# Moving a recurrence's gate units from the attention phase to the scans, with one weight pool and weights laid out by group

## The chip, the cores and the metric

The kernel runs on one core of a Trainium2 chip, with its engines TensorE (PE, with its weight loads PEld), VectorE (DVE), ScalarE (ACT), GpSimd (POOL) and SyncE (SP). Each engine takes its instructions in order; SP issues every DMA of this kernel, one behind the other. The metric is the time of one execution on the device, in microseconds (us).

## The reference, cut to what matters

One layer over 2048 tokens (32 rows of 64) of width 1024, with 256 context tokens:

```python
h  = rms_norm(x, norm_g) * (1 + scale) + shift          # hc likewise for the context
q, k, v, z_a, u, z_l = split(h @ w_in, 6 parts of 512)   # w_in: 1024 x 3072
attn = neighbourhood_attention(rope(q), q, rope(k), v, k_c, v_c, rpb)   # 8 heads of 64
uc = depthwise_conv(u); ucc = depthwise_conv(u_c)        # width 4
y  = scan_forward + scan_backward of the RG-LRU          # a, b from gates of uc (64 x 64 blocks)
mix = concat([attn * silu(z_a), y * silu(z_l)]) @ w_out
out = x + gate * mix
```

The gate of the recurrence is silu(z_l), the last 512 columns of w_in; its product with y is what this change moves.

## The kernel before, in words

Float32 products are made of three float16 matmuls: the prepared tokens stand as hh (high) and hl (low), four blocks of 512 tokens each; a group of weights is loaded as float32 (raw, name wraw), its largest value found (L319, and allmax L111 to L116, which crosses the partitions by two small matmuls on PE), scaled by a power of two and split into wh (ACT, L324) and wl (DVE, L325). A projection with 128 channels on the partitions (proj_ct, L344 to L346) is 8 x 3 matmuls of 512 columns.

Phase 1 (phase1): modulation vectors, preparation of x and context (prep_in, prep), the tables of the attention's bias (tables: rp is multiplied, stored as d_r, spread to d_f, copied by ACT as te, d_t, and stored as d_e), the u projections (u_proj, with the convolution L364 to L381 on DVE), and then lru for channel groups c = 0 to 3 of 128 channels. lru makes, for two directions, the gates (L447 to L449 on PE in 5 pieces of tokens, tanh L451), exp, tanh and sqrt (L455 to L458), a product (L459) and the scan (L461 forwards, L468 backwards in three pieces); POOL adds the directions (L471) and d_y stores y (L472). Between the directions, fill runs units of the attention's gate z_a: silu_z (24 projections, tanh L479, product sz L480) and four stores d_z.

Phase 2 (phase2): heads 0 to 6, each in four quarters t (steps 4n + t), with the projections of the next head beside (proj_tc, L602 to L604). Between steps stand the units of the recurrence's gate (lru_gate): load y, silu_z, four products ry (L995, L997), store d_re. The table LU says behind which steps a unit stands; `later(LZ)` gives a unit a later priority. Head 7 and the output projection follow.

The order on each engine is settled before the run by a scheduler that goes through the program's instructions by priority and takes the earliest that its own model finds ready; pools of tiles (bufs = number of buffers of a tag) make an instruction wait for the last reader of its buffer.

In the profile PE's duration of one matmul is longer than its distance to the next one, since they overlap.

Of the kernel before, what the change touches and what calls it, by code (L numbers as in the profile page):

```python
# [17 lines left out]
D = 1024  # L18
# [13 lines left out]
CQ, CK, CV, CZA, CU, CZL = 0, 512, 1024, 1536, 2048, 2560  # L32
# [19 lines left out]
LZ = 80  # L52

LU = (0, 2, 4, 6, 8, 10, 12, 14, 16, 18, 20, 22, 24, 25, 26, 27)
# [4 lines left out]
class K:  # L59
# [93 lines left out]
    def mods(self, p):  # L153
# [20 lines left out]
        for i in range(2):  # L174
            for k in range(KC):
                w = p.tile([128, D], F32, tag="x", name="wm", bufs=12)
# [77 lines left out]
    def prep_in(self, p, src, n, tb=None):  # L254
# [37 lines left out]
    def w_tiles(self, tag, n):  # L292

        if tag == "z":
            return [self.wp["z"].tile([128, KC, 128], F16, tag=x, name=x, bufs=3) for x in ("wh", "wl")]
        if tag == "l":
            return [self.wp["l"].tile([128, KC, 128], F16, tag=x, name=x, bufs=1) for x in ("wh", "wl")]
        return [self.wp["h"].tile([128, KC, 192], F16, tag=x, name=x, bufs=2)[:, :, 0:n] for x in ("wh", "wl")]

    def wload(self, parts, tag):  # L300

        n = sum(w for _, w in parts)
        wp = self.wp["z" if tag == "z" else "h"]
        if tag == "z":
            raw = wp.tile([128, KC, n], F32, tag="raw", name="wraw", bufs=2)
        else:
            raw = wp.tile([128, KC, 192], F32, tag="raw", name="wraw", bufs=1)[:, :, 0:n]
        wv = self.a["w_in"].rearrange("(k p) n -> p k n", p=128)
        o = 0
        for c, w in parts:  # L310
            self.nc.sync.dma_start(raw[:, :, o:o + w], wv[:, :, c:c + w])
            o += w
        return raw, n, tag

    def wsplit(self, raw, n, tag, early=False):
# [7 lines left out]
        wh, wl = self.w_tiles(tag, n)  # L323
# [8 lines left out]
    def wgroup(self, parts, tag, slow=False, early=False):  # L332
        raw = self.wload(parts, tag)
# [77 lines left out]
    def lru(self, c, uc, p, fill):  # L411
# [54 lines left out]
        for o, m in ((0, CTX), (CTX + S // 2, S // 2), (CTX, S // 2)):  # L466
# [3 lines left out]
            if o:  # L470
                nc.gpsimd.tensor_tensor(F[:, o:o + m], A[:, o:o + m], F[:, o:o + m], ALU.add)  # L471
                nc.sync.dma_start(self.d_y[128 * c:128 * c + 128, o - CTX:o - CTX + m], F[:, o:o + m])  # L472
# [10 lines left out]
    def phase1(self, left, right):  # L483
# [7 lines left out]
        self.zp = self.pool(right, "z", side="right")  # L491
        self.wright = right.enter_context(ExitStack())
        self.zs = self.const.tile([128, 8], F32, name="zs")
        self.wp = {}
# [3 lines left out]
        with ExitStack() as s1:  # L498
            self.wp["z"] = self.pool(s1, "w1", bufs=2)
# [3 lines left out]
            def u_group(c, g=None):  # L503
                wh, wl, osc = g or self.wgroup([(CU + 128 * c, 128)], "z", slow=c > 1)
# [16 lines left out]
            with ExitStack() as s0:  # L521
# [3 lines left out]
                with self.tc.issue_after(self.last.ins):  # L525
                    g0 = self.wgroup([(CU, 128)], "z", early=True)
# [17 lines left out]
            za = []  # L544

            def z_group():
                c = len(za)
                g = self.wgroup([(CZA + 128 * c, 128)], "z", slow=c > 0)
                nc.vector.tensor_scalar(self.zs[:, c:c + 1], g[2], 0.5, None, ALU.mult)
                za.append(g)  # L550
            with ExitStack() as s2:
                p = self.pool(s2, "lru")
                ug[2] = u_group(2)
                z_group()

                def z_units(c, d):
                    wh, wl, _ = za[c]
                    for tb in (2 * d, 2 * d + 1):
                        z = self.silu_z(self.zp, self.bank("mm"), wh, wl, self.zs[:, c:c + 1], tb)
                        dz = self.d_z[c][tb].rearrange("p (j f x) -> p f j x", j=4, f=2)  # L560
                        for f in range(2):
                            zf = z[:, 256 * f:256 * f + 256]
                            nc.sync.dma_start(dz[:, f, 0:3], zf[:, 32:224].rearrange("p (j x) -> p j x", j=3))
                            nc.sync.dma_start(dz[:, f, 3].rearrange("p (e x) -> p e x", e=2),
                                              bass.AP(zf.tensor, zf.offset, [list(zf.ap[0]), [224, 2], [1, 32]]))
                    if d == 0 and c < 3:
                        z_group()

                for c in range(4):
                    self.lru(c, ucs[c], p, lambda d, c=c: z_units(c, d))  # L570
                    if c < 2:
                        ucs.append(u_proj(c + 2))
            self.wp["h"] = self.pool(self.wright, "w2", bufs=2, side="right")
# [156 lines left out]
    def head_w(self, n):  # L730
        return self.wload([(CQ + HD * n, HD), (CK + HD * n, HD), (CV + HD * n, HD)], "h")
# [188 lines left out]
    def phase2(self, left, right):  # L920
# [4 lines left out]
        self.wp["l"] = self.pool(self.wright, "w3", side="right")  # L925
        with ExitStack() as sg:
# [22 lines left out]
            lz = self.lru_gate()  # L949
            next(lz)  # L950
            for n in range(NH - 1):
                nxt = self.head_proj(n + 1, p, q)
                for t, _ in enumerate(self.attention(n, H, p)):
# [5 lines left out]
                    step = 4 * n + t  # L959
                    if step in LU:  # L960
                        next(lz)
                    if LU.index(step + 1) % 4 == 0 if step + 1 in LU else False:
                        next(lz)
# [5 lines left out]
            next(lz, None)  # L969
# [3 lines left out]
    def lru_gate(self):  # L973

        nc = self.nc
        for c in range(4):
            hsc = self.zs[:, 4 + c:5 + c]

            raw = self.wload([(CZL + 128 * c, 128)], "h" if c == 3 else "l")
            yield  # L980
            wh, wl, osc = self.wsplit(*raw)
            nc.vector.tensor_scalar(hsc, osc, 0.5, None, ALU.mult)
            for tb in range(4):
                with self.later(LZ):
                    y = self.wp["l"].tile([128, 512], F32, tag="y", name="y", bufs=1)
                    nc.sync.dma_start(y, self.d_y[128 * c:128 * c + 128, 512 * tb:512 * tb + 512])
                    z = self.silu_z(self.zp, self.bank("mm"), wh, wl, hsc, tb)
                    w1 = self.zp.tile([128, 512], F32, tag="z", name="ry", bufs=2)
                    for f in range(2):
                        s = slice(256 * f, 256 * f + 256)  # L990
                        yf = y[:, s].rearrange("p (r c) -> p c r", r=4)
                        zf = z[:, s].rearrange("p (c r) -> p c r", r=4)
                        wf = w1.rearrange("p (i f c r) -> p f i c r", i=4, f=2, r=4)[:, f]
                        iv = lambda x: x[:, 8:56].rearrange("p (i c) r -> p i c r", i=3)
                        nc.vector.tensor_tensor(wf[:, 0:3], iv(zf), iv(yf), ALU.mult)  # L995
                        ev = lambda x: bass.AP(x.tensor, x.offset, [list(x.ap[0]), [56 * x.ap[1][0], 2], [x.ap[1][0], 8], list(x.ap[2])])
                        nc.vector.tensor_tensor(wf[:, 3].rearrange("p (e c) r -> p e c r", e=2), ev(zf), ev(yf), ALU.mult)  # L997
                    nc.sync.dma_start(self.d_re[tb][128 * c:128 * c + 128, :], w1)
                yield


    def room(self):

        return self.wp["h"].tile([128, KC, 192], F32, tag="raw", name="wo", bufs=1).rearrange("p k n -> p (k n)")[:, 0:D]
# [135 lines left out]
```

## Time and profile before

| | |
|---|---|
| median of 3 runs | 1279.6 us (1273.95 to 1280.06) |
| profiled execution | 1277.88 us, its span 1276.1 us |
| mean granted TensorE clock | 0.936 of full speed |
| PE busy | 1122.0 us (88%) |
| DVE busy | 926.6 us (73%) |
| ACT busy | 615.2 us (48%) |
| POOL busy | 478.7 us (38%) |

Busy times are sums over the span; how far an engine limits the kernel differs by stage, so the rows below take the span apart. The 40 slices of the page (31.9 us each) show PE's busy share in tenths:

```profile
PE   7777889689981879999999999999999976999997
DVE  7798655989775677888978989798887863544432
```

The scans begin in slice 7 and end in slice 13; the attention of heads 0 to 6 fills slices 14 to 33.

### The profile page before, as it was taken

Reading aid. Unit: us, or ns where it says so; the run is one execution under the profiler, and the core shown is the slowest. Engines: PE = TensorE matmul, PEld = TensorE weight load, DVE = VectorE, ACT = ScalarE, POOL = GpSimd, SP = SyncE. Lnnn points to the kernel's source line nnn. Section 1 sums busy time; section 2 is a strip of 40 time slices with the busy share of each in tenths; the row PEclk is TensorE's granted clock in tenths of the full one; section 3 lists DMA queues with packets and bytes.
Section 4 is the critical chain, followed back from the end, with each engine's and each line's share of the span. In section 5 each row is a group of like instructions: output and inputs, shape, how many; then the busy total and the mean of one; then the engine's idle time right before and its main releaser. Section 6 shows DMA issues by size and latency. Waiting matters only on the chain. (4 is left out here: it accounts for less than half of the span.)

```text
span 1276.1 us, 26205 instructions
## 1 busy us (share of the span) xinstructions
PE 1122.0 (88%) x9964; PEld 858.8 (67%) x9964; DVE 926.6 (73%) x2546; ACT 615.2 (48%) x1189; POOL 478.7 (38%) x863
## 2 busy tenths in 40 slices
PE   7777889689981879999999999999999976999997
PEld 1434345445540767889878898788887755778786
DVE  7798655989775677888978989798887863544432
ACT  1597116876773225555655555555556452231210
POOL 0144002234122087566566556565564552000000
PEclk9788899699996889999999999999999997999999
DMA  9846980011024414344543435334354346346452
GB/s 349 284 153 237 312 250 26 4 50 54 17 67 99 93 34 85 83 97 96 118 88 83 95 86 137 82 89 76 86 129 103 89 99 177 95 134 176 122 149 83
DMA packets 196014, 149.50 MB, mean 117 GB/s; under 512 B 129453, under 2 KB 168109, under 8 KB 195887
## 3 DMA queue, kind: packets, MB, share of 16 engines
q1 hardware_dynamic: 195887, 147.82, 43.3%
q8 instruction: 78, 1.28, 0.4%
q14 instruction: 49, 0.40, 0.1%
HBM read 96.42 MB, written 47.94 MB: 113 GB/s over the span
## 5 line engine op out<-in xcount | busy, mean ns | idle before, releaser
L602 PE MATMUL mm<-wh,hh 128*128 128x192 f16 x960 | 236.9, 247 | 0.0
L603 PE MATMUL mm<-wl,hh 128*128 128x192 f16 x960 | 236.9, 247 | 0.0
L604 PE MATMUL mm<-wh,hl 128*128 128x192 f16 x960 | 236.9, 247 | 0.0
L893 DVE TENSOR_TENSOR Pl<-pt,Ph 128x384 f16<-128x384 f32 (+1 forms) x256 | 127.4, 516 | 56.2 <-ACT Ph L892 55.7
L344 PE MATMUL mm<-hh,wh 128*128 128x512 f16 x384 | 150.3, 392 | 12.9 <-DVE sz L480 7.6
L345 PE MATMUL mm<-hl,wh 128*128 128x512 f16 x384 | 149.2, 389 | 8.3 <-POOL hl L289 7.9
L885 ACT ACTIVATE SP<-SP,nb 128x640 f32<-128x640 f32 (+1 forms) x128 | 110.7, 881 | 91.9 <-DVE nb L883 87.7
L346 PE MATMUL mm<-hh,wl 128*128 128x512 f16 x384 | 149.0, 388 | 0.0
L892 ACT CAST Ph<-pt 128x384 f16<-128x384 f32 (+1 forms) x256 | 107.1, 453 | 67.5 <-PE pt L891 66.6
L891 PE MATMUL pt<-id,SP 128*128 128x128 f32 x704 | 115.6, 282 | 0.6 <-ACT SP L885 0.2
L602 PEld LDWEIGHTS <-hh 128*128 128x128 f16 x1024 | 100.6, 98 | 3.6 <-issue 2.8
L603 PEld LDWEIGHTS <-hh 128*128 128x128 f16 x1024 | 100.5, 98 | 1.8 <-issue 0.3
L604 PEld LDWEIGHTS <-hl 128*128 128x128 f16 x1024 | 100.5, 98 | 1.0
L880 DVE CUSTOM_DVE_ANT_0 SP<-sl,b,m 128x384 f32<-128x384 f32 (+1 forms) x128 | 93.2, 735 | 6.6 <-PE sl L828 4.5
L828 PE MATMUL sl<-qk,qt 128*128 128x128 f16 (+2 forms) x800 | 78.2, 230 | 16.9 <-DVE m L880 6.9
L898 PEld LDWEIGHTS <-Ph 128*128 128x128 f16 x1408 | 79.1, 97 | 9.9 <-ACT Ph L892 3.1
L891 PEld LDWEIGHTS pt<-id,SP 128*128 128x128 f32 x704 | 78.9, 143 | 5.2 <-ACT SP L885 1.2
L443 POOL TENSOR_TENSOR ul<-uc,uh 128x512 fp32r<-128x512 f32 (+1 forms) x20 | 33.0, 1679 | 123.3 <-ACT uh L442 123.3
L346 PEld LDWEIGHTS <-wl 128*128 128x128 f16 x416 | 41.6, 100 | 55.4 <-issue 16.9
L717 POOL TENSOR_TENSOR ST<-P,ST 128x256 f16<-128x256 f32 x64 | 43.4, 679 | 93.7 <-ACT ST L716 93.2
L898 PEld LDWEIGHTS <-Pl 128*128 128x128 f16 x704 | 65.8, 98 | 16.1 <-DVE Pl L893 9.8
L345 PEld LDWEIGHTS <-wh 128*128 128x128 f16 x416 | 41.9, 101 | 50.3 <-issue 14.0
(303 smaller groups left out, 3060.9 us busy)
## 6 DMA issues: line engine op xcount, KB each, us to landing
b<-d_e SPq DMA_DIRECT2D x32, 288.0 KB
wm<-w_mod SPq DMA_DIRECT2D x16, 512.0 KB
x<-x SPq DMA_DIRECT2D x16, 512.0 KB
wraw<-w_in SPq DMA_DIRECT2D x12, 512.0 KB
d_t<-te SPq DMA_DIRECT2D x12, 512.0 KB
d_e<-d_t SPq DMA_DIRECT2D x8, 768.0 KB
wraw<-w_in SPq DMA_DIRECT2D x24, 256.0 KB
b<-d_e SPq DMA_DIRECT2D x16, 384.0 KB
```

The costliest lines, as they stand in the source:

```text
L344: nc.tensor.matmul(out, wh[:, k, :], hh[:, k, :n], start=(k == 0), stop=False)
L345: nc.tensor.matmul(out, wh[:, k, :], hl[:, k, :n], start=False, stop=False)
L346: nc.tensor.matmul(out, wl[:, k, :], hh[:, k, :n], start=False, stop=(k == KC - 1))
L602: nc.tensor.matmul(out, hh[:, k, t0:t0 + 128], wh[:, k, :], start=(k == 0), stop=False)
L603: nc.tensor.matmul(out, hh[:, k, t0:t0 + 128], wl[:, k, :], start=False, stop=False)
L604: nc.tensor.matmul(out, hl[:, k, t0:t0 + 128], wh[:, k, :], start=False, stop=(k == KC - 1))
L880: nc.vector.tensor_tensor_reduce(SP[:, 0:W], sl[:, 0:W], bt[:, CT[j], 0:W], self.qs, m1, ALU.add, ALU.max, accum_out=m2)
L885: nc.scalar.activation(SP[:, :N], SP[:, :N], AF.Exp, bias=nb)
L891: nc.tensor.transpose(pt[:, i - c0, :], SP[:, 128 * i:128 * i + 128], self.id32)
L892: nc.scalar.copy(Ph[:, c0:c1], pt)
L893: nc.vector.tensor_tensor(Pl[:, c0:c1], pt, Ph[:, c0:c1], ALU.subtract)
L898: nc.tensor.matmul(pv[:, jj], P[:, i, :], v[:, w:w + 66], start=(i == j0 == 0), stop=(i == nch - 1 and j0 == 2))
```

## The change

- lru_gate(c, tb, wh, wl) is now one unit, called from fill in phase 1: fill(c, d) runs z_unit(c, tb) for two blocks and, from group 1 on, lru_gate(c − 1, tb) for the same blocks. The four units of group 3 follow behind lru(3). LU, LZ and their calls in phase 2 are gone.
- The weights of z_a, u, z_l and of the heads come from one pool, w: raw has one buffer, wh and wl three, all of 8 x 192 columns. Before, phase 1 had raw two and wh, wl three (8 x 128), phase 2 one and two, and the gate's units their own.
- The host lays w_in out as w_gr (12 groups of 128 columns: each partition has one row of 4 KB) and w_qkv (8 heads: one row of 6 KB); a head's weights are one DMA in place of three.
- d_y is one tile per group; y and ry have a pool of their own with one buffer each; x and wm have 11 buffers, not 12.
- In the code, u group 3's weights and the z groups are asked for behind lru(c), and the first z_a group without the wait of slow.

```diff
-LZ = 80
-LU = (0, 2, 4, 6, 8, 10, 12, 14, 16, 18, 20, 22, 24, 25, 26, 27)
...
-        self.d_y = d.tile([LW, S], F32, name="d_y")
+        self.d_y = [d.tile([128, S], F32, name=f"d_y{c}") for c in range(4)]
...
-            x = p.tile([128, D], F32, tag="x", name="x", bufs=12)
+            x = p.tile([128, D], F32, tag="x", name="x", bufs=11)
...
+    def wload(self, src):
+        n = src.shape[2]
+        raw = self.wp.tile([128, KC * 192], F32, tag="raw", name="wraw", bufs=1)[:, 0:KC * n].rearrange("p (k n) -> p k n", k=KC)
+        self.nc.sync.dma_start(raw, src)
+        return raw, n
...
+        wh, wl = [self.wp.tile([128, KC * 192], F16, tag=x, name=x, bufs=3)[:, 0:KC * n].rearrange("p (k n) -> p k n", k=KC)
+                  for x in ("wh", "wl")]
...
+            def z_group(gs, k0, slow=True):
+                c = len(gs)
+                g = self.wgroup((GZL if k0 else GZA) + c, slow=slow)
+                nc.vector.tensor_scalar(self.zs[:, k0 + c:k0 + c + 1], g[2], 0.5, None, ALU.mult)
+                gs.append(g)
...
+                ug[2] = u_group(2)
+                z_group(za, 0, False)
+                def fill(c, d):
                     for tb in (2 * d, 2 * d + 1):
+                        z_unit(c, tb)
+                        if c:
+                            self.lru_gate(c - 1, tb, *zl[c - 1][:2])
                 for c in range(4):
+                    self.lru(c, ucs[c], p, lambda d, c=c: fill(c, d))
                     if c < 2:
                         ucs.append(u_proj(c + 2))
+                    if c < 3:
+                        z_group(za, 0)
+                        if c == 0:
+                            ug[3] = u_group(3)
+                        z_group(zl, 4)
+            z_group(zl, 4)
+            for tb in range(4):
+                self.lru_gate(3, tb, *zl[3][:2])
+            zright.close()
...
     def head_w(self, n):
-        return self.wload([(CQ + HD * n, HD), (CK + HD * n, HD), (CV + HD * n, HD)], "h")
+        return self.wload(self.a["w_qkv"][n])
...
-                    step = 4 * n + t
-                    if step in LU:
-                        next(lz)
-                    if LU.index(step + 1) % 4 == 0 if step + 1 in LU else False:
-                        next(lz)
...
+    def lru_gate(self, c, tb, wh, wl):
+        y = self.yp.tile([128, 512], F32, tag="y", name="y", bufs=1)
+        nc.sync.dma_start(y, self.d_y[c][:, 512 * tb:512 * tb + 512])
+        z = self.silu_z(self.zp, self.bank("mm"), wh, wl, self.zs[:, 4 + c:5 + c], tb)
+        w1 = self.yp.tile([128, 512], F32, tag="ry", name="ry", bufs=1)
...
+    w = np.asarray(inputs["w_in"]).reshape(KC, 128, 3 * D).transpose(1, 0, 2)
+    arrays["w_qkv"] = np.ascontiguousarray(w[:, :, :3 * AW].reshape(128, KC, 3, NH, HD).transpose(3, 0, 1, 2, 4).reshape(NH, 128, KC, 3 * HD))
+    arrays["w_gr"] = np.ascontiguousarray(w[:, :, 3 * AW:].reshape(128, KC, 12, 128).transpose(2, 0, 1, 3))
```

In the order of instructions the change shows at two places. First, VectorE where group 2 ends and group 3 begins. Before (L452 is the first product of a group's gates, L468 the backward scan of group 2, L480 a unit's sz):

```order
L480 SCALAR_TENSOR_TENSOR sz<-sz,mm 128x512
L459 TENSOR_TENSOR X<-X,I 128x2304
L480 SCALAR_TENSOR_TENSOR sz<-sz,mm 128x512
L452 SCALAR_TENSOR_TENSOR I<-I,uc 128x256
L452 SCALAR_TENSOR_TENSOR I<-I,uc 128x512
L468 SCALAR_TENSOR_TENSOR A<-A,X 128x256
L468 SCALAR_TENSOR_TENSOR A<-A,X 128x1024 x2
L452 SCALAR_TENSOR_TENSOR I<-I,uc 128x512 x3
```

The L452 rows around the scan belong to group 3, whose first gates are already done. After, with lines 18 lower (L450 is the scan, L462 sz, L351 the convolution of a u group, L300 the largest weight):

```order
L462 SCALAR_TENSOR_TENSOR sz<-sz,mm 128x512
L450 SCALAR_TENSOR_TENSOR A<-A,X 128x256
L450 SCALAR_TENSOR_TENSOR A<-A,X 128x1024 x2
L300 TENSOR_REDUCE wm<-wraw 128x1
L462 SCALAR_TENSOR_TENSOR sz<-sz,mm 128x512
L110 TENSOR_REDUCE av<-po 1x1
L973 TENSOR_TENSOR ry<-sz,y 128x3x64
L975 TENSOR_TENSOR ry<-sz,y 128x64
L973 TENSOR_TENSOR ry<-sz,y 128x3x64
L975 TENSOR_TENSOR ry<-sz,y 128x64
L351 SCALAR_TENSOR_TENSOR uc<-mm,cw_2042,uc 128x255
L357 COPY cy_2532<-mm 128x1
```

Behind the scan of group 2 now stands the convolution of u group 3; the first L434 (the product L452 of before) of group 3 comes 70 rows further down, and on PE 288 projections of 512 columns and 24 of 256 stand between the last gate of group 2 and the first of group 3.

Second, SP behind the last stores of y. Before (y and z are loads, b the tables' loads, wraw a head's weights):

```order
L472 DMA d_y<-A 128x1024 x2
L931 DMA rope<-rope 128x768
L311 DMA wraw<-w_in 128x8x64 x3
L690 DMA b<-d_e_1025 64x1152 x2
L690 DMA b<-d_e_1026 64x1536 x2
L986 DMA y<-d_y 128x512
L843 DMA z<-d_z_68 128x512
L311 DMA wraw<-w_in 128x8x64 x3
```

After:

```order
L926 DMA rope<-rope 128x768
L686 DMA b<-d_e_1028 64x1152
L293 DMA wraw<-w_qkv 128x1536
L686 DMA b<-d_e_1028 64x1152
L686 DMA b<-d_e_1029 64x1536 x2
L839 DMA z<-d_z_68 128x512
L976 DMA d_re_91<-ry 128x512
L964 DMA y<-d_y_95 128x512
L976 DMA d_re_88<-ry 128x512
L964 DMA y<-d_y_95 128x512
```

The loads of y and the stores d_re of groups 2 and 3 now stand between the loads for head 0 and the weights of head 1.

## Rows read from the trace of the kernel before

**Rows 1.** Windows by stage: span, busy us, (instructions) of each engine, clock, DMA share.

```profile
0.00:207.50 207.50, 163.75 (x696) 77.48 (x697) 149.22 (x356) 91.57 (x150) 46.44 (x51) 0.88 0.75 247
207.50:420.10 212.60, 156.48 (x682) 89.51 (x681) 167.46 (x175) 144.90 (x180) 53.57 (x52) 0.85 0.19 50
420.10:1052.00 631.90, 598.84 (x7474) 528.22 (x7474) 519.12 (x1838) 334.05 (x778) 367.73 (x752) 0.98 0.41 91
```

**Rows 2.** Windows, channel groups 0 to 3 and the stretch to head 0.

```profile
207.50:262.10 54.60, 40.97 (x163) 26.51 (x162) 47.97 (x60) 41.78 (x56) 11.70 (x7) 0.81 0.05 15
262.10:312.90 50.80, 44.41 (x204) 25.37 (x203) 43.69 (x39) 37.76 (x47) 17.31 (x8) 0.90 0.17 45
312.90:362.70 49.80, 47.77 (x220) 25.48 (x219) 40.50 (x44) 36.44 (x48) 11.67 (x7) 1.00 0.13 32
362.70:401.70 39.00, 22.17 (x96) 11.47 (x93) 31.88 (x22) 27.35 (x28) 7.07 (x3) 0.83 0.20 54
401.70:420.10 18.40, 1.16 (x4) 0.68 (x5) 3.41 (x13) 1.57 (x1) 5.83 (x29) 0.50 0.85 209
```

**Rows 3.** Timeline of PE: start, duration, line, tiles, [idle before <-releaser].

```profile
206.96 0.47 PE L447 MATMUL sl<-uh,gh 128*128 128x256 f32 x1
...
339.76 0.40 PE L449 MATMUL sc<-uh,gl 128*128 128x512 f32 x1
...
382.14 0.39 PE L449 MATMUL sc<-uh,gl 128*128 128x512 f32 x1
382.37 0.39 PE L345 MATMUL mm<-hl,wh 128*128 128x512 f16 x1
...
387.78 0.38 PE L346 MATMUL mm<-hh,wl 128*128 128x512 f16 x1
...
420.14 0.26 PE L602 MATMUL sl<-wh,hhc 128*128 128x128 f16 x1 [2.42 <-ACT wh L324]
```

**Rows 4.** Timeline of DVE around the last scans of groups 2 and 3.

```profile
357.22 5.46 DVE L468 TENSOR_TENSOR_SCAN A<-A,X 128x256 f32<-128x256 f32 x3
...
396.24 5.46 DVE L468 TENSOR_TENSOR_SCAN A<-A,X 128x256 f32<-128x256 f32 x3
414.38 1.75 DVE L319 TENSOR_REDUCE wm<-wraw 128x1 f32<-128x1536 f32 x1 [12.68 <-DMA wraw<-w_in]
...
417.75 0.16 DVE L116 COPY am<-mm 128x1 f32<-128x1 f32 x1 [0.67 <-PE mm L114]
```

**Rows 5.** Timeline of SP behind the last scan: DMA issues.

```profile
407.05 3.29 SPq L311 DMA_DIRECT2D wraw<-w_in  x3
...
413.34 0.53 SPq L986 DMA_DIRECT2D y<-d_y  x1
```

**Rows 6.** Windows, the 12 steps of phase 2 without a unit: their sum.

```profile
sum 220.59, PE 213.60 PEld 196.07 DVE 179.63 ACT 118.91 POOL 114.15; mean PE 17.80 PEld 16.34 DVE 14.97 ACT 9.91 POOL 9.51
```

**Rows 7.** The same for the 15 steps with a unit.

```profile
sum 316.09, PE 308.90 PEld 263.33 DVE 272.03 ACT 180.51 POOL 202.53; mean PE 20.59 PEld 17.56 DVE 18.14 ACT 12.03 POOL 13.50
```

**Rows 8.** Lines of DVE, 420 to 1052 us: count | busy us, mean ns | idle before.

```profile
L995 DVE TENSOR_TENSOR ry<-sz,y 128x192 f32<-128x192 f32 x32 | 21.7, 678 | 0.0
...
L997 DVE TENSOR_TENSOR ry<-sz,y 128x64 f32<-128x64 f32 x32 | 15.4, 483 | 0.0
...
L480 DVE SCALAR_TENSOR_TENSOR sz<-sz,mm 128x512 f32<-128x512 f32 x16 | 10.8, 677 | 0.0
```

**Rows 9.** Timeline of DVE, the tables' first product and block 0.

```profile
50.82 0.62 DVE L632 TENSOR_SCALAR rp<-rp,acols 120x31 f32<-120x31 f32 x1
...
64.86 0.41 DVE L287 CAST hh<-h 128x512 f16<-128x512 f32 x1
```

**Rows 10.** Lines of DVE, 207 to 420 us: the convolution of two u groups.

```profile
L369 DVE SCALAR_TENSOR_TENSOR uc<-us,cw,uc 128x512 f32<-128x512 f32 (+2 forms) x24 | 22.9, 958 | 0.2
...
L364 DVE TENSOR_SCALAR uc<-us,cw,vec 128x512 f32<-128x512 f32 x8 | 7.5, 953 | 0.7 <-ACT us L362 0.6
```

**Rows 11.** The chain of waits: start, us, what it waited for.

```profile
1124.11 3.27 DMA m<-d_at
```

More of the change, by code (lines that the diff above doesn't have):

```diff
@@ L289, in prep, with wsplit @@
             self.hl_op = eng.tensor_tensor(hl[:, k, :], h[:, :m], hh[:, k, :], ALU.subtract)
[L292 to L315, printed above, removed]
+    def wload(self, src):
[3 more added lines that the diff above has]
+        return raw, n
+    def wsplit(self, raw, n, early=False):
         nc = self.nc
@@ L330, in wsplit, with wgroup @@
         return wh, wl, osc
-    def wgroup(self, parts, tag, slow=False, early=False):
-        raw = self.wload(parts, tag)
+    def wgroup(self, g, slow=False, early=False):
+        raw = self.wload(self.a["w_gr"][g])
         with ExitStack() as st:
@@ L471, in lru @@
                 nc.gpsimd.tensor_tensor(F[:, o:o + m], A[:, o:o + m], F[:, o:o + m], ALU.add)
-                nc.sync.dma_start(self.d_y[128 * c:128 * c + 128, o - CTX:o - CTX + m], F[:, o:o + m])
+                nc.sync.dma_start(self.d_y[c][:, o - CTX:o - CTX + m], F[:, o:o + m])
     def silu_z(self, p, pz, wh, wl, hsc, tb):
@@ new lines, in z_unit @@
+            def z_unit(c, tb):
+                z = self.silu_z(self.zp, self.bank("mm"), *za[c][:2], self.zs[:, c:c + 1], tb)
+                dz = self.d_z[c][tb].rearrange("p (j f x) -> p f j x", j=4, f=2)
+                for f in range(2):
+                    zf = z[:, 256 * f:256 * f + 256]
+                    nc.sync.dma_start(dz[:, f, 0:3], zf[:, 32:224].rearrange("p (j x) -> p j x", j=3))
+                    nc.sync.dma_start(dz[:, f, 3].rearrange("p (e x) -> p e x", e=2),
+                                      bass.AP(zf.tensor, zf.offset, [list(zf.ap[0]), [224, 2], [1, 32]]))
@@ L551, in phase1 @@
             with ExitStack() as s2:
                 p = self.pool(s2, "lru")
+                self.yp = self.pool(zright, "y", side="right")
                 ug[2] = u_group(2)
-                z_group()
-                def z_units(c, d):
-                    wh, wl, _ = za[c]
+                z_group(za, 0, False)
+                def fill(c, d):
                     for tb in (2 * d, 2 * d + 1):
[L559 to L567, printed above, removed]
+                        z_unit(c, tb)
+                        if c:
+                            self.lru_gate(c - 1, tb, *zl[c - 1][:2])
@@ L968, in phase2 @@
             self.out_weights(range(4, 8), self.room)
-            next(lz, None)
         self.wright.close()
         return self.attention(NH - 1, H, p)
-    def lru_gate(self):
+    def lru_gate(self, c, tb, wh, wl):
         nc = self.nc
[L976 to L999, printed above, removed]
@@ new lines, in lru_gate @@
+        y = self.yp.tile([128, 512], F32, tag="y", name="y", bufs=1)
+        nc.sync.dma_start(y, self.d_y[c][:, 512 * tb:512 * tb + 512])
+        z = self.silu_z(self.zp, self.bank("mm"), wh, wl, self.zs[:, 4 + c:5 + c], tb)
+        w1 = self.yp.tile([128, 512], F32, tag="ry", name="ry", bufs=1)
+        for f in range(2):
+            s = slice(256 * f, 256 * f + 256)
+            yf = y[:, s].rearrange("p (r c) -> p c r", r=4)
+            zf = z[:, s].rearrange("p (c r) -> p c r", r=4)
+            wf = w1.rearrange("p (i f c r) -> p f i c r", i=4, f=2, r=4)[:, f]
+            iv = lambda x: x[:, 8:56].rearrange("p (i c) r -> p i c r", i=3)
+            nc.vector.tensor_tensor(wf[:, 0:3], iv(zf), iv(yf), ALU.mult)
+            ev = lambda x: bass.AP(x.tensor, x.offset, [list(x.ap[0]), [56 * x.ap[1][0], 2], [x.ap[1][0], 8], list(x.ap[2])])
+            nc.vector.tensor_tensor(wf[:, 3].rearrange("p (e c) r -> p e c r", e=2), ev(zf), ev(yf), ALU.mult)
@@ L1002, in room @@
+        nc.sync.dma_start(self.d_re[tb][128 * c:128 * c + 128, :], w1)
     def room(self):
-        return self.wp["h"].tile([128, KC, 192], F32, tag="raw", name="wo", bufs=1).rearrange("p k n -> p (k n)")[:, 0:D]
+        return self.wp.tile([128, KC * 192], F32, tag="raw", name="wo", bufs=1)[:, 0:D]
     def out_weights(self, ks, room):
```

29 lines of the change are left out of this document (9 added, 20 removed).

## The prediction

> **What bounds the kernel now.** I read the busy time by stage first. From the first gate of the recurrence (about 207 us) to the first projection of head 0 (420.1 us) TensorE is busy 156.48 of 212.60 us and VectorE 167.46. In the attention of heads 0 to 6 (420 to 1052) TensorE is busy 598.84 of 631.90 [rows 1]. So the attention is bound by TensorE, and the stage of the scans is bound by neither: there the three engines wait for each other. The same view by channel group shows where TensorE idles [rows 2]: 13.6, 6.4, 2.0 and 16.8 us in groups 0 to 3, then 17.2 of the 18.4 us between the last scan and head 0. Second, the timeline of TensorE: a gate matmul of 512 columns takes 0.23 us to the next instruction (382.14 to 382.37), projections of 512 columns follow each other every 0.216 us (25 of them from 382.37 to 387.78) [rows 3]. One unit of a recurrence gate is 24 such projections, 5.2 us; the 16 units together are 384, or 82.9 us. Third, VectorE's timeline: the last scan of group 2 ends at 362.7 and of group 3 at 401.7, and after that head 0 waits for its weights to land (12.68 us) and for their split [rows 4]. SP issues those weights at 407.05, behind the last stores of y [rows 5].
>
> **What phase 2 gives back.** The table puts a unit into 15 of the 27 whole (head, quarter) steps that follow the first. Step by step from the second reciprocal of one (L901) to that of the next, the 12 steps without a unit have TensorE busy 213.60 of 220.59 us (6.99 idle) and the 15 steps with one 308.90 of 316.09 (7.19 idle) [rows 6, 7]. Idle per step is 0.58 without and 0.48 with. The units fill no idle time here, they lengthen the phase, so without them it is shorter by nearly all of 82.9 us. I take off 3 us for 15 steps that become a little worse: **−80**. The bounds are −86 (VectorE, busy 519 of 632 us there [rows 1], also loses L995, L997 and L480, 47.9 us [rows 8]) and −48, which is VectorE's share alone, if VectorE turned out to pace these steps.
>
> **What the scans' stage now carries.** Four steps.
>
> *Up to the first gate: +3 (from −5 to +16).* The x tiles have 11 buffers in place of 12, and the raw weights one in place of two. The product rp, whose store d_r opens the chain of the bias tables, ran on VectorE at 50.82 us, before block 0 of the prepared x; in the new order it stands behind the third cast of that block, which ended at 65.3 [rows 9], and d_r stands on SP behind x tiles that wait for buffers: some 14 to 18 us later, 16 by the middle. The tables are not read before head 0, but ScalarE copies them (te) between its other work. I pass on 3 of the 16 and keep 16 as the upper bound; below, 5 us, since the last loads wg and the store d_g now stand earlier on SP. Weights in rows of 4 KB in place of 512 B can only land sooner; the one wait for weights that these rows show is head 0's, so I count nothing for it here.
>
> *First gate to the last gate of group 2: 0 (from −16 to +7).* It was 206.96 to 340.15 us [rows 3], 133.2. VectorE is busy 132.2 of the 155 us of groups 0 to 2 [rows 2]. It loses the convolution of u group 3 (22.9 + 7.5 us for two groups [rows 10], so 15.2), which now stands behind the scans of group 2. It gains three ry products with their sz (2.3 + 0.7 us each, from the sums of [rows 8] over 16 units) and two splits of weights of about 3 us: 15 us. Even, therefore. The low bound has VectorE busy 95% of this stretch in place of 85 (139 us against 155), the high one 82% as in group 3.
>
> *Last gate of group 2 to the last scan of group 3: +69 (from +64 to +77).* Before, it was 340.15 to 401.7, 61.5 us. In the order after, 288 projections of 512 columns and 24 of 256 stand on TensorE between the last gate of group 2 and the first of group 3: u group 3, which used to stand in front of those gates, and eight units. 288 x 0.216 + 24 x 0.11 = 64.8 us, with no gate in them, so neither ScalarE nor VectorE can begin group 3. Between this gate and the last gate of group 3 stand 168 more: 36.3 us, and the 60 gate matmuls take 12.3. Then tanh, exp, sqrt, product and scan, which took 19.2 us from 382.5 to 401.7; I take 17, since one sz fewer stands among them. Sum 130.4, against 61.5. It is paced by TensorE, so waits can only add, up to 8 us as I take it from the 16.8 idle of group 3 before; the low end is a chain of 12 us in place of 17 behind the last gate.
>
> *Last scan to head 0: +21 (from +15 to +25).* It was 18.4 us [rows 2]. Now the split of head 0's weights stands on VectorE behind the last ry, and the units of group 3 stand behind a wait. Their largest weight is reduced (av) only after the last scan, so their first projection starts about 8 us after it; four units take 20.8, so TensorE is through at +29. The ry chain runs beside it: y has one buffer and ry one, so each round is product 2.3, issue of d_re and y 0.4 each, landing 3.3 (a quarter-megabyte load of d_at took 3.27 [rows 11]): 6.4 us. y(3,0) is issued behind d_y, rope, the tables b, the head's weights and d_re(2,3), at about +11, and lands between +14.4 and +18.4 behind the head's weights, which took 7.3 us [rows 5, 4]; I take +16. Product, three more rounds and the split (2.4 us from L116 to the first projection [rows 4, 3]): 16 + 2.3 + 19.2 + 2.4 = 39.9. Loading the head's weights by one DMA in place of three saves 2.9 of 3.29 us on SP, which is in the +11. The tiles d_y by group take no wait away that a row shows.
>
> Sum: +3 + 0 + 69 + 21 − 80 = **+13** on the profiled execution (span 1276.1 and 1.8 us around it, 1277.9), 1291. The median of the runs is 1.7 above that, so 1292. In other words: 82.9 us of units, and 69 projections of 512 and 24 of 256 columns of u groups that used to stand in front of the first gate (17.5 us), come into a stage that grows by 90 us, so only some 10 of its 56 us of idle time are filled: the units stand in one lump and at the tail, not in the gaps.
>
> **Rivals.**
>
> *Faster: the units sink into the idle time.* TensorE idles 56 us between 207.5 and 420.1, 39 of it beside the scans [rows 1, 2]. If its order lets 39 of the 82.9 us sink in, and the tail stays at 18.4, head 0 starts 44 later, and −80 makes it −36: about 1244. For it: group 0 and group 3 have 13.6 and 16.8 us of idle that a unit could take without moving a gate. Against it: group 2 has only 2.0 left, and the stretch without gates lies just behind it. The Trainium skill, "Perfetto Trace Analysis", section "Optimization Strategy", says of kernels whose most contended engine changes over time that interleaving the regimes may help. By that rule this is the case to expect; the trace bears out its premise (rows 1 show the two regimes), but not that these gaps are where the order puts the units.
>
> *No change: denser scans.* VectorE, relieved of u group 3, runs groups 0 to 2 at its low bound, −16 in place of 0. Then the sum is −3, about 1277.
>
> *Slower: the late tables pass through.* If the store d_r and ScalarE's copies te, which stand in order before later copies of the prepared x, hold up the prepared blocks, the first gate is 16 late rather than 3, and the sum is +26: 1306. It decides if the first gate starts after about 220 us. For it: x buffers and raw buffers both shrink on the stage whose DMA engines are busiest (share 0.75 up to 207.5 us, against 0.19 beside the scans [rows 1]).
>
> *Slower: phase 2 gives back only VectorE's share.* −48 in place of −80 gives +45, 1325. Against it stand rows 6 and 7.
>
> **How the numbers follow.** A measurement of this kernel tells changes of about 0.5% (6.4 us) from none. Forecast 0.50, of which 0.38 lie above 1286 and 0.12 within the band, since its terms together can move by some 13 us; the units sink in 0.27 (0.25 faster, 0.02 same); denser scans 0.06 (same); late tables 0.12 and VectorE's share 0.05 (both slower). Slower 0.55, same 0.20, faster 0.25. The likeliest case has its own range, 1278 to 1304; for 8 in 10 I reach from 1251, part of the way to the faster rival, to 1310, past the late tables.
>
> **What would show it.** In the profile after: the first gate near 210; the last gate of group 2 near 344; a stretch of about 65 us on TensorE of projections alone at over 95% busy, and the first gate of group 3 behind it; the last scan near 474; 36 to 42 us from there to the first projection of head 0, near 513, with y and d_re in turns of about 6 us on SP; and then 856 − 80 us to the end with TensorE's share in the attention as before. The forecast is wrong if head 0 starts before 495, if TensorE's idle time between the first gate and head 0 is under 40 us, or if phase 2 shrinks by less than 70.

## The result, and the profile after

The changed kernel is slower: 1316.5 us median (1313.2 to 1318.8, 4 runs) against 1279.0, ratio 1.030 (95% interval 1.026 to 1.034). The forecast was 1292 and its range ended at 1310. The direction was right, the size was not: the profiled span grew by 35.3 us (1276.1 to 1311.4), the sum said 13.

Windows of the kernel after, cut at the same events as the terms of the sum: up to the first gate, to the last gate of group 2, to the last scan, to head 0, and the attention from the end of its first step to the end of the 28th (columns as in [rows 1]):

```profile
0.00:211.20 211.20, 140.33 (x589) 65.64 (x590) 136.32 (x327) 87.58 (x143) 46.17 (x51) 0.83 0.69 233
211.20:337.70 126.50, 103.12 (x437) 59.90 (x436) 104.18 (x127) 94.85 (x121) 32.17 (x16) 0.89 0.15 46
337.70:479.30 141.60, 135.04 (x624) 65.59 (x623) 95.18 (x146) 65.31 (x79) 14.82 (x8) 0.98 0.26 73
479.30:523.20 43.90, 29.82 (x130) 12.76 (x129) 20.54 (x54) 6.73 (x8) 6.06 (x29) 0.90 0.57 161
...
600.00:1067.90 467.90, 438.34 (x6152) 418.54 (x6151) 408.55 (x1495) 282.51 (x674) 297.02 (x633) 0.99 0.40 88
```

TensorE is idle 23.4 + 6.6 + 14.1 = 44 us from the first gate to head 0, near the forecast (46). Head 0 starts at 523.2 in place of 420.1: +103.1, where +93 was expected. What follows takes 788.2 in place of 856.0: −67.8, where −80 was expected. The last window has 29.6 us of idle TensorE; the same stretch before had 14.2 of 536.7.

TensorE's timeline shows the long stretch. L431 at 337.27 is the last gate of group 2, L429 at 408.80 the first of group 3, L431 at 463.55 its last, L598 the first projection of head 0:

```profile
337.27 0.40 PE L431 MATMUL sc<-uh,gl 128*128 128x512 f32 x1
...
347.56 0.58 PE L326 MATMUL mm<-hh,wh 128*128 128x512 f16 x1 [4.70 <-DVE sz L462]
...
408.80 0.47 PE L429 MATMUL sl<-uh,gh 128*128 128x256 f32 x1
...
409.23 0.39 PE L326 MATMUL mm<-hh,wh 128*128 128x512 f16 x1
...
414.20 0.38 PE L328 MATMUL mm<-hh,wl 128*128 128x512 f16 x1
...
463.55 0.39 PE L431 MATMUL sc<-uh,gl 128*128 128x512 f32 x1
...
523.18 0.26 PE L598 MATMUL sl<-wh,hhc 128*128 128x128 f16 x1 [6.66 <-ACT wh L306]
```

Between the two gates lie 71.5 us, and behind the first two matmuls of group 3's first gate another whole unit (409.23 to 414.2) stands in front of the third. VectorE's timeline of the tail: the last scan, the reduction of group 3's weights (av), head 0's weights (wm), and the first product ry of the first, second and fourth unit of group 3:

```profile
474.54 4.74 DVE L450 TENSOR_TENSOR_SCAN A<-A,X 128x1024 f32<-128x1024 f32 x2
479.19 0.25 DVE L110 TENSOR_REDUCE av<-po 1x1 f32<-1x128 f32 x1
...
498.77 1.75 DVE L300 TENSOR_REDUCE wm<-wraw 128x1 f32<-128x1536 f32 x1 [8.02 <-DMA wraw<-w_qkv]
...
504.78 0.49 DVE L973 TENSOR_TENSOR ry<-sz,y 128x192 f32<-128x192 f32 x1 [3.66 <-DMA y<-d_y]
...
509.67 0.49 DVE L973 TENSOR_TENSOR ry<-sz,y 128x192 f32<-128x192 f32 x1 [3.04 <-DMA y<-d_y]
...
519.85 0.49 DVE L973 TENSOR_TENSOR ry<-sz,y 128x192 f32<-128x192 f32 x1 [3.09 <-DMA y<-d_y]
```

SP issued head 0's weights at 490.26 and the first y of group 3 at 494.72:

```profile
490.26 0.52 SPq L293 DMA_DIRECT2D wraw<-w_qkv  x1
...
494.72 0.42 SPq L964 DMA_DIRECT2D y<-d_y  x1
...
506.49 0.37 SPq L964 DMA_DIRECT2D y<-d_y  x1
```

That y was used at 504.78, ten us after its issue, which followed those of the tables and of head 0's weights; the later ones 3.2 to 3.5 us after theirs.

### The profile page after: what moved, and what is told of

The parts are those of the page before. It is cut to its first block, busy times and chain, and to the rows that moved or that the text cites. A ratio compares the mean times of both kernels' runs of the same rounds, so it can differ in the third digit from the quotient of the medians.

```text
span 1311.4 us, 26189 instructions
## 1 busy us (share of the span) xinstructions
PE 1126.9 (86%) x9964; PEld 857.5 (65%) x9964; DVE 925.3 (71%) x2546; ACT 616.0 (47%) x1189; POOL 463.8 (35%) x863
## 3 DMA queue, kind: packets, MB, share of 16 engines
q8 instruction: 78, 1.28, 0.4%
## 5 line engine op out<-in xcount | busy, mean ns | idle before, releaser
L598 PE MATMUL mm<-wh,hh 128*128 128x192 f16 x960 | 236.6, 246 | 2.9 <-DVE V L756 1.9
L328 PE MATMUL mm<-hh,wl 128*128 128x512 f16 x384 | 149.9, 391 | 0.8 <-DVE wl L307 0.7
L888 ACT CAST Ph<-pt 128x384 f16<-128x384 f32 (+1 forms) x256 | 110.3, 452 | 76.2 <-PE pt L887 73.1
L887 PE MATMUL pt<-id,SP 128*128 128x128 f32 x704 | 119.4, 283 | 6.3 <-DVE Pl L889 5.8
L598 PEld LDWEIGHTS <-hh 128*128 128x128 f16 x1024 | 100.3, 98 | 7.5 <-issue 6.9
L327 PEld LDWEIGHTS <-wh 128*128 128x128 f16 x416 | 41.9, 101 | 64.6 <-issue 26.3
L824 PEld LDWEIGHTS <-qt 128*128 128x128 f16 x800 | 57.6, 100 | 33.5 <-issue 27.5
L453 POOL TENSOR_TENSOR A<-A 128x1024 f32<-128x1024 f32 x8 | 24.0, 3013 | 155.9 <-issue 82.2
L326 PEld LDWEIGHTS <-wh 128*128 128x128 f16 x416 | 42.1, 101 | 55.1 <-issue 9.5
```

The lines of the kernel that those rows point to most:

```text
L326: nc.tensor.matmul(out, wh[:, k, :], hh[:, k, :n], start=(k == 0), stop=False)
L327: nc.tensor.matmul(out, wh[:, k, :], hl[:, k, :n], start=False, stop=False)
L328: nc.tensor.matmul(out, wl[:, k, :], hh[:, k, :n], start=False, stop=(k == KC - 1))
L598: nc.tensor.matmul(out, hh[:, k, t0:t0 + 128], wh[:, k, :], start=(k == 0), stop=False)
L824: self.nc.tensor.matmul(out, lq, k(x[:, i]), start=(i == 2), stop=(i == 3))
L887: nc.tensor.transpose(pt[:, i - c0, :], SP[:, 128 * i:128 * i + 128], self.id32)
```

## The experiments

Columns of windows are as in [rows 1]; ratios are against the kernel before, with their 95% intervals. Line numbers shift by a few between kernels.

**Without the units, kernel before.** The calls in phase 2 are taken out, and with them the loads of the units' weights; the output projection reads d_y, so the gate of the recurrence is left out.

```diff
-            lz = self.lru_gate()
-            next(lz)
...
-                    if step in LU:
-                        next(lz)
...
-        src = (self.d_re if h else self.d_at)[tb]...
+        src = (self.d_y[:, 512 * tb:512 * tb + 512] if h else self.d_at[tb])...
```

Expected: 

> The kernel before without the 16 units of the recurrence's gate (their projections, products and stores are left out, and the output projection reads y as the scans stored it); nothing else is changed. Theory A, the units' absence itself exposes waits in the attention: phase 2 gives back some 68 us here too, not 80; about 1211 us, with TensorE idle some 25 to 30 us between the end of the first step and the end of the last (14.2 before). Rival B, the other edits of the change (one weight pool, one raw buffer, order on SP) cost those 12 us: about 1199 us, idle 14 as before.

Measured: 1207.8 us, ratio 0.945 (0.942 to 0.948). Theory A. Nothing but the units and their weights is gone, head 0 starts at 420.0 as before, and the attention from the first to the 28th step takes 467.0 us, as in the changed kernel (467.9):

```profile
205.50:420.00 214.50, 158.25 (x686) 90.78 (x685) 167.48 (x176) 145.00 (x180) 53.55 (x52) 0.84 0.19 50
...
499.60:966.60 467.00, 439.27 (x6145) 419.67 (x6143) 404.80 (x1495) 282.43 (x675) 301.17 (x638) 0.98 0.42 89
```

It is 69.7 shorter than before, with TensorE idle 27.7 us. The waits of TensorE in that stretch, before (total us, times, longest):

```profile
PE po L898 <- DVE Pl L893: 4.0, 8, 0.9
...
PE sl L828 <- DMA qk<-ST: 0.7, 2, 0.4
```

after the change:

```profile
PE sl L824 <- DMA qk<-ST: 10.8, 6, 3.5
PE pt L887 <- DVE Pl L889: 5.8, 5, 3.3
```

and before without units:

```profile
PE sl L829 <- DMA qk<-ST: 8.3, 5, 2.9
PE po L899 <- DVE Pl L894: 5.5, 8, 1.6
PE pt L892 <- DVE Pl L894: 5.1, 4, 2.8
```

The wait for qk, the transposed queries and keys of the next head, grows from 0.7 to 10.8 and 8.3 us. The waits for Pl, the low half of the attention's weights, were 4.0 us before and grow to 10.6 in the first run. I read it so: those loads and products were in time before because TensorE had units to do meanwhile. That taking the units out brings the waits is shown, since nothing else was changed in the code; how much of it is the missing work and how much the order, which the scheduler settles anew, is not.

**Layout alone.** The kernel before, weights by group and one DMA per head.

```diff
-            self.nc.sync.dma_start(raw[:, :, o:o + w], wv[:, :, c:c + w])
+        self.nc.sync.dma_start(raw, self.a["w_qkv"][c // HD] if len(parts) == 3 else self.a["w_gr"][(c - CZA) // 128])
```

Expected: 

> The kernel before with the weights of the input projection laid out by group and one DMA per head in place of three; pools, places and order as before. Theory: 1273 to 1283, no change, since only head 0's weights are waited for long; at most 3 us earlier there. Rival, rows of 256 and 512 bytes cost much: 1270 or less.

Measured: 1285.3 us, ratio 1.006 (1.004 to 1.009): neither theory. Up to head 0 it is equal (420.1); the attention takes 543.0 us in place of 536.7. See the tenth run.

**Without the units, kernel after.**

```diff
-                        if c:
-                            self.lru_gate(c - 1, tb, *zl[c - 1][:2])
...
-            for tb in range(4):
-                self.lru_gate(3, tb, *zl[3][:2])
```

The four groups of the units' weights are not loaded either, and the output projection reads the tiles d_y.

Expected: 

> The changed kernel without the 16 units (same work left out as in the first run). Theory A: within 6 us of the first run, 1205 to 1217; the other edits are neutral once the units are gone. Rival B, pool, x buffers and late tables cost time by themselves: 1220 or more.

Measured: 1208.9 us, ratio 0.945 (0.942 to 0.948), theory A: without the units the other edits together cost nothing that can be told. They are not neutral one by one, though. The last scan ends at 414.5 in place of 401.6 in the first run, and the stretch behind it is 2.3 us in place of 18.4:

```profile
414.50:416.80 2.30, 0.00 (x0) 0.00 (x0) 2.16 (x7) 1.57 (x1) 2.18 (x1) 0.50 0.15 62
```

So, with 1277.0 for the kernel before beside these runs, 16 units cost 1277.0 − 1207.8 = 69 us in the attention and 1316.5 − 1208.9 = 108 us beside the scans of the changed kernel, where TensorE's work for them is 83.

**Two raw buffers, four of wh and wl.** The changed kernel; phase 1's weights have a pool of 128 columns, the heads' weights one of their own behind it.

```diff
...
-        self.wp = self.pool(self.wright, "w", side="right")
...
+        self.wp, self.wn, self.wb = self.pool(zright, "w1", side="right"), 128, (2, 4)
...
             zright.close()
+            self.wp, self.wn, self.wb = self.pool(self.wright, "w2", side="right"), 192, (1, 2)
```

(wn is the width of a tile's columns, wb the numbers of buffers.)

Expected: 

> The changed kernel with two raw buffers and four of wh and wl in phase 1 (in a pool of 128 columns), and a pool of its own for the heads' weights; the units stay beside the scans. Theory C, one raw buffer and three of wh and wl push u group 3 and the units of group 1 behind the gates of group 2, which makes the stretch of 71 us without gates: that stretch goes, the last scan comes 20 to 35 us earlier and the time is 1283 to 1298. Rival D, the stretch is set by the scans' own order (y comes late) and not by weights: 1312 to 1320.

Measured: 1267.5 us, ratio 0.991 (0.988 to 0.994): below theory C's range, in its direction. It is 49 us under the changed kernel and faster than the kernel before. The last scan ends 41 us earlier where 20 to 35 were expected, and from the last gate of group 2 to the first of group 3 it takes 8.6 us in place of 71.5. The windows up to the first gate, the last gate of group 2, the last scan and head 0, and the attention:

```profile
0.00:201.30 201.30, 155.72 (x698) 72.51 (x699) 144.40 (x351) 91.69 (x150) 47.90 (x50) 0.93 0.75 254
201.30:366.90 165.60, 141.87 (x630) 79.42 (x631) 131.78 (x177) 105.20 (x136) 31.11 (x17) 0.93 0.19 55
366.90:438.30 71.40, 69.74 (x325) 35.18 (x323) 56.15 (x76) 49.45 (x57) 15.87 (x8) 1.00 0.26 71
438.30:485.20 46.90, 28.05 (x127) 12.38 (x126) 20.45 (x52) 6.62 (x8) 6.14 (x29) 0.87 0.52 150
...
563.00:1026.30 463.30, 438.05 (x6153) 416.69 (x6151) 406.76 (x1499) 283.76 (x679) 301.80 (x639) 0.99 0.42 89
```

**Two raw, three of wh and wl** (`(2, 3)` in the same line).

Expected: 

> As the last run (two raw buffers, four of wh and wl), with three of wh and wl as in the kernel before and after. Theory C1, the one raw buffer alone is the cause: 1264 to 1275, as with four. Theory C2, wh and wl are what lacks: 1300 or more. If the units were slow whatever the buffers (theory D): 1312 or more.

Measured: 1271.3 us, ratio 0.995 (0.993 to 0.996): C1. Head 0 starts at 477.7, 7.5 us before the fourth run's, and the attention is 11 us longer (474.4 for 463.3).

**One raw, four of wh and wl** (`(1, 4)`).

Expected: 

> One raw buffer as in the changed kernel, four of wh and wl. Theory C1: 1305 to 1320, with the stretch without gates behind group 2 still 60 us or longer. Theory C2: 1264 to 1280.

Measured: 1309.2 us, ratio 1.026 (1.024 to 1.028): C1 again; from the last gate of group 2 to the first of group 3 it takes 68.7 us. The same first four windows:

```profile
0.00:210.90 210.90, 138.12 (x589) 64.72 (x590) 137.79 (x327) 87.71 (x143) 46.02 (x51) 0.84 0.69 234
210.90:341.30 130.40, 103.30 (x437) 59.45 (x436) 102.87 (x128) 96.62 (x122) 33.16 (x16) 0.87 0.15 47
341.30:480.10 138.80, 133.39 (x624) 64.93 (x623) 96.10 (x145) 63.01 (x78) 12.82 (x8) 0.99 0.26 72
480.10:524.90 44.80, 28.43 (x129) 12.55 (x128) 20.89 (x54) 6.73 (x8) 6.12 (x29) 0.88 0.54 157
```

The fourth and the sixth run differ in the raw buffer alone: 1309.2 − 1267.5 = 42 us. Head 0 moves by 39.7 us of it (524.9 to 485.2). In front of the first gate TensorE is idle 72.8 us with one buffer and 45.6 with two: these 27.2 us are most of it. 4.6 us more of idle time lie behind the first gate; the other 7.9 are longer busy time, which is not taken apart here. The first gate itself comes only 9.6 us later (210.9 for 201.3), since less work stands in front of it: 288 projections of 512 columns with one buffer and 360 with two, 72 x 0.216 = 15.6 us, and 24 narrow ones fewer. They stand behind it instead. How one buffer does it is seen on SP. In the kernel before, d_r went at

```profile
51.47 0.35 SPq L634 DMA_DIRECT2D d_r<-rp  x1
```

and after the change, with the third and the fourth load of weights,

```profile
64.50 0.33 SPq L293 DMA_DIRECT2D wraw<-w_gr  x1
69.39 0.35 SPq L630 DMA_DIRECT2D d_r<-rp  x1
...
168.16 0.34 SPq L293 DMA_DIRECT2D wraw<-w_gr  x1
```

on VectorE, after the change (the splits of the second and the third load):

```profile
63.19 1.28 DVE L307 SCALAR_TENSOR_TENSOR wl<-wraw,ws,wh 128x1024 f16<-128x1024 f32 x1
...
139.08 1.28 DVE L307 SCALAR_TENSOR_TENSOR wl<-wraw,ws,wh 128x1024 f16<-128x1024 f32 x1
```

on TensorE, after the change (a step of the fourth load's largest value, and the first projection with these weights):

```profile
179.48 0.37 PE L108 MATMUL po<-id,wm 128*1 128x128 f32 x1 [27.46 <-DVE wm L300]
...
185.99 0.61 PE L326 MATMUL mm<-hh,wh 128*128 128x512 f16 x1 [3.36 <-ACT wh L306]
```

and on SP with two raw and three of wh and wl, and the same 11 buffers of x, the third and the fourth load:

```profile
41.09 0.34 SPq L293 DMA_DIRECT2D wraw<-w_gr  x1
...
49.77 0.34 SPq L631 DMA_DIRECT2D d_r<-rp  x1
51.03 0.34 SPq L293 DMA_DIRECT2D wraw<-w_gr  x1
```

With one raw buffer a load waits for the split before it. The third (u group 2) is issued at 64.50, as the split wl of the second ends (63.19 + 1.28), in place of 41.09. The fourth (group 0 of z_a) cannot go before the third's split ends at 140.4; it goes at 168.16, behind the tables' stores d_e on SP (128.5 to 164.6), in place of 51.03. Up to 179.48 TensorE stands idle for 27.46 us, waiting for these weights. The four units of z_a begin at 185.99 and fill it up to the first gate, and u group 2 is projected from 214.2 on, behind that gate; in the fifth run, with two raw buffers, the units of z_a begin at 149.9 and u group 2 at 176.4, in front of it. So what is late is the fourth load, and u group 2, whose weights are split by 140.4, stands behind it in the order. d_r waits for rp, which VectorE runs at 69.12 in this order; with two raw buffers d_r goes at 49.77, so the 11 x buffers are not what delayed the tables.

**Two buffers of y** (on top of the fourth run).

```diff
-        y = self.yp.tile([128, 512], F32, tag="y", name="y", bufs=1)
+        y = self.yp.tile([128, 512], F32, tag="y", name="y", bufs=2)
```

Expected: 

> Two raw buffers, four of wh and wl, and two buffers of y in place of one. Theory E, the rounds of y load, product and store set the 47 us between the last scan and head 0: with two buffers the loads run ahead, some 10 us less there, 1255 to 1261. Rival, head 0's weights or the projections of the units behind end just as late: 1264 to 1270.

Measured: 1268.1 us, ratio 0.993 (0.990 to 0.996): the rival. From the last scan to head 0 it takes 43.1 us in place of 46.9; head 0 starts only 1.4 us earlier (483.8), so the rounds alone do not set it.

**Group 3 back in the attention** (on top of the fourth run; steps 8, 10, 12, 14). Here and in the last three runs the units in the attention load their weights there, as in the kernel before, and have their pools there.

Expected: 

> Two raw buffers, four of wh and wl, and the four units of group 3 back in the attention (steps 8, 10, 12, 14), those of groups 0 to 2 beside the scans. Theory F, a unit costs 69/16 = 4.3 us in the attention, and group 3's chain costs some 25 us between the last scan and head 0: -25 + 17 = 1255 to 1263. Rival, the chain of group 2's units takes its place: 1267 to 1280.

Measured: 1268.9 us, ratio 0.994 (0.991 to 0.996). The theory's range is missed, the rival's holds: 27.5 us still lie between the last scan and head 0 (441.6 to 469.1), now with group 2's units. Head 0 starts 16 us earlier than in the fourth run (469.1 for 485.2), the attention is 17 us longer (480.6 for 463.3): four units cost the same in either place.

**One raw buffer in the kernel before.**

```diff
-            raw = wp.tile([128, KC, n], F32, tag="raw", name="wraw", bufs=2)
+            raw = wp.tile([128, KC, n], F32, tag="raw", name="wraw", bufs=1)
```

Expected: 

> The kernel before with one raw buffer in phase 1 in place of two, and nothing else; the units stay in the attention. Theory C1, the one raw buffer does the harm by itself: u group 2's 72 projections (15.6 us) and 24 narrow ones leave the idle time in front of the first gate, which comes 4 to 10 us later; head 0 starts 15 to 30 us later, 1292 to 1308. Rival, it harms only together with the moved units, which ask for four more groups of weights: 1276 to 1284.

Measured: 1287.2 us, ratio 1.008 (1.005 to 1.012), between the two. The first gate comes at 208.1, 1.1 us later and not 4 to 10, and head 0 at 430.8, 10.7 later; the stretch behind the last scan is 19.0 us.

So one raw buffer costs 10 us in the kernel before and 42 in the changed kernel (sixth against fourth run), where twelve groups of weights in place of eight pass through it in phase 1. That the number of groups makes the difference is my reading; no run changes it alone.

**The old layout, two raw and four of wh and wl.**

```diff
-        self.nc.sync.dma_start(raw, src)
+        for c, w in src:
+            self.nc.sync.dma_start(raw[:, :, o:o + w], wv[:, :, c:c + w])
+            o += w
```

Expected: 

> Two raw buffers and four of wh and wl, units beside the scans, with the weights read from w_in as before (rows of 512 and 256 bytes, three DMAs per head). Theory G, the layout by group is what made the second run 0.6% slower: 1258 to 1264, some 6 us under the version with it. Rival, that was another order of phase 2 that the scheduler happened to settle: 1264 to 1272.

Measured: 1282.8 us, ratio 1.005 (1.003 to 1.007): 15 us slower than with the layout by group, the opposite of the second run and outside both ranges. Head 0 starts within 1.4 us of the fourth run; 10 us lie in the attention (473.3 for 463.3), where the wait for qk is 14.2 us:

```profile
PE sl L829 <- DMA qk<-ST: 14.2, 7, 4.1
```

Among the eight versions without units in the attention that stretch took 463.3 to 474.4 us, with nearly the same instructions in it. What of this is the layout and what the order that the scheduler settled is open.

**Only group 0 beside the scans** (two raw, four of wh and wl; G1 = 1, and the other twelve units at steps 8 to 27).

```diff
+                        if c and c <= G1:
+                            self.lru_gate(c - 1, tb, *zl[c - 1][:2])
```

Expected: 

> Two raw buffers, four of wh and wl; only group 0's four units beside the scans, the other twelve in the attention. Theory H, what counts is idle time that a unit can fill: beside groups 1 to 3 TensorE has 25 us free before, so four units cost nothing there and save 4 x 4.3: 1258 to 1264. Rival, the gain came from all units leaving the attention together: 1270 to 1278.

Measured: 1260.5 us, ratio 0.986 (0.983 to 0.990), the lowest median of all, faster than both kernels. The attention:

```profile
494.20:1013.30 519.10, 497.57 (x6434) 443.74 (x6432) 440.18 (x1578) 294.61 (x691) 310.83 (x642) 1.00 0.41 95
```

The time is in theory H's range, but not by its mechanism. The attention is 17.6 us shorter, 4.4 a unit, as expected. The units are not free, though: the last scan comes at 412.0 in place of 401.7, with the first gate 5.7 us earlier. That head 0 still starts at 414.2 (420.1 before) is because the 18.4 us behind the last scan have become 2.2. Whether the place of the units or the pools made the gain, the last run tells.

**Groups 0 and 1 beside the scans.**

Expected: 

> The same with groups 0 and 1 beside the scans and groups 2 and 3 in the attention. Theory H: eight units fill more than the free time, but group 2's and 3's chains are gone from the stretch before head 0: 1255 to 1265, the best of the split versions. Rival: as with group 3 alone in the attention, 1266 to 1272.

Measured: 1264.1 us, ratio 0.989 (0.985 to 0.992): in theory H's range, with the same doubt. It was expected to be the best of the split versions, and by its median it is not.

**All units in the attention, the other edits kept** (two raw, four of wh and wl; G1 = 0, the steps of the kernel before).

Expected: 

> Two raw buffers, four of wh and wl, all sixteen units in the attention as in the kernel before (same steps); the other edits of the change stay. It tells what moving units is worth when weights have buffers. Theory I, the gain of the version with group 0 beside the scans came from its place (four units cost little there and save 17 us in the attention): 1272 to 1280. Rival J, it came from the weights: first gate 6 us earlier and head 0's weights issued ahead of the last scan, and the four units only paid for themselves: 1256 to 1264.

Measured: 1263.1 us, ratio 0.989 (0.986 to 0.993): rival J. No unit is moved, and the time is that of the versions with four or eight units moved (0.986 and 0.989). Windows from the last scan to head 0, and of the attention:

```profile
403.40:405.70 2.30, 0.02 (x1) 0.02 (x1) 2.13 (x9) 1.57 (x1) 2.30 (x2) 0.50 0.00 0
...
484.60:1019.20 534.60, 518.89 (x6574) 455.64 (x6573) 450.58 (x1604) 299.92 (x696) 316.01 (x643) 1.00 0.42 98
```

The attention is nearly as long as before (534.6 for 536.7 us), and head 0 starts at 405.7, 14.4 us earlier, all of it behind the last scan: 2.3 us in place of 18.4. The first gate comes 4.2 us earlier, but the last scan 1.7 later, so of rival J's two reasons the second alone is borne out. SP issues head 0's weights at 392.59, ahead of the last stores of y, where the kernel before issued them at 407.05 behind them [rows 5]:

```profile
392.59 0.42 SPq L296 DMA_DIRECT2D wraw<-w_qkv  x1
...
405.58 2.62 SPq L457 DMA_DIRECT2D d_y<-A  x2
```

Why they go earlier (memory that comes free sooner, or the scheduler's order) was not tried. It is not the number of raw buffers: the third run, with one, has the same short stretch. The layout alone does not do it either: in the second run the stretch is 19.0 us. Against this version, moving all sixteen units (the fourth run, 0.991) gains nothing: head 0 starts 79.5 us later (485.2) and the attention is 71.3 us shorter (463.3). This is a second pair with and without units in the attention, and TensorE's idle time there grows again (15.7 to 25.3 us).

## Why the prediction missed

Point by point, with the terms of the profiled execution:

- Up to the first gate, +3: measured +4.2, right by luck. The tables came 18 us late (d_r at 69.39 in place of 51.47), as foreseen, but the x buffers, one of the two reasons named, were not it: with two raw buffers and 11 of x d_r goes at 49.77. What held TensorE up was the wait of 27.46 us for weights, and on weights the prediction says "I count nothing for it here", since the rows showed no such wait; the rows came from a kernel with two raw buffers. With two, the changed kernel has its first gate at 201.3, 5.7 us before the old one, so this wait and the other edits happened to leave +4.2. The rival of the late tables did not happen: the first gate is not after 220.
- First gate to the last gate of group 2, 0: measured −6.7, inside its bounds.
- To the last scan, +69: measured +80.1, above its bound. 5.2 of the miss is a unit that I counted in neither piece: 24 projections inside the first gate's three matmuls (409.23 to 414.2). 4.7 is a wait of a unit for sz (347.56). The mechanism, a lump of projections without gates, was right, but it belongs to the one raw buffer: in the fourth run the lump is gone.
- Last scan to head 0, +21: measured +25.5, just above its bound. y landed at +25.5 and not +16 after the scan, ten us behind its issue; rounds of 5.0 in place of 6.4 us gave half of that back.
- **Phase 2, −80: measured −67.8**, less than the 70 that the prediction itself named as a sign of being wrong. This is the step that failed most: "The units fill no idle time here, they lengthen the phase". Rows 6 and 7 compared steps with a unit and steps without one *in the same kernel*. Those steps did not differ by a unit alone: TensorE is busy 20.59 us in the mean with one and 17.80 without, a difference of 2.79 where a unit is 5.2. The steps without one also stood beside steps with one, and may have profited from the slack that these gave to the loads of qk; that is not shown. Taken out everywhere, the first run gives back 69.7 in the attention, and TensorE's idle time there doubles (14.2 to 27.7 us). None of the eight versions without units there gives back 80: it is 62 to 73, and what sets the place in this range is open.

Together the terms missed by 22 us. What the sum did not price by itself is the cause of the loss: one raw buffer in place of two stood in the +3, and its effects, which the order showed, stood in the other terms as if they belonged to moving the units. By the fourth and sixth run it costs 42 us. Moving the units is worth nothing that can be told once weights have their buffers: 1267.5 us with all sixteen moved, 1263.1 with none.

The rival "the units sink into the idle time" holds only in part even with two raw buffers: TensorE is idle 44 us between first gate and head 0 in the fourth run and 37 in the fifth, against 56 before. The Trainium skill, "Perfetto Trace Analysis", section "Optimization Strategy", says that interleaving regimes may help where the most-contended engine changes over time, and also that a gap which repeats on the engine that should be saturated can mean too few buffers. The runs do not bear out the first here (the fourth against the last run). Of the second they show another form: one buffer too few cost 42 us, most of it as one wait of 27.46 us, not as a repeating gap.

## What to carry to other kernels

Price filler work by taking it out everywhere, not by comparing stretches with and without it in one kernel. When a change moves work and shrinks a pool, price the two apart: here the pool made the loss, and with its buffers back the move itself was worth nothing. When a version wins, run it once without the part that is supposed to win.

## What the runs showed that I had not expected

A load of 256 KB of y took 3.2 to 3.5 us from issue to use when only a store d_re was issued just before it, and 10.1 us behind the tables and a head's weights (494.72 to 504.78). The stretch between the last scan and head 0, 18.4 us in the kernel before, went to 2.3 us without an edit meant for it, and that is the larger part of what the best versions gain. It did so in the third run too, where it made up for a last scan that came 13 us later, so that two effects of 13 and 16 us looked like none.
